# A split-precision feed-forward on one TensorE: within a weight tile, all products with the high parts first, then all with the low parts

## The chip, the core and the metric

The kernel runs on one core of one Trainium2 chip. The metric is the device time of one execution in microseconds (us). TensorE does the matrix products (PE in the profile; PEld is its weight load), VectorE is DVE, ScalarE is ACT, GpSimd is POOL, and SyncE (SP) issues most DMAs.

## The reference, cut to what matters

One layer of a hybrid model is computed for 128 context tokens and 512 latent tokens, 640 columns in all. The change lies in its last two pieces, the output projection and the feed-forward block:

```python
x = x + g1 * (jnp.concatenate([o_a, o_b], axis=-1) @ lp['w_out'])
h = _rmsnorm(x, lp['norm2_g']) * (1.0 + sc2) + sh2
ff = (jax.nn.silu(h @ lp['w_ffn_gate']) * (h @ lp['w_ffn_up'])) @ lp['w_ffn_down']
return x + g2 * ff, s_fin
```

The model width is 2048 and the feed-forward width is 5632. All inputs and outputs are 32-bit floats.

## The kernel before

**A product in three.** Each float matrix is split into a high part (a cast to the 32-bit format fp32r, in which TensorE takes it) and a low part (the matrix minus its high part). A product is the sum of three: high weight by high operand, high weight by low operand, low weight by high operand. The helper `parts` makes the weight's two parts: ACT casts `raw` to `hi` (line 1423), and DVE subtracts to get `lo` (line 1424). It does that once for a weight tile of `nk` blocks of 128x128 (`nk` is 4, or 3 in the first two chunks of the down projection). `hi`, `lo` and the sums `t3` of weights lie in the pool `st`, with three buffers each: a fourth `hi` can be written only when TensorE has read the first.

**Stages.** The output projection runs as two passes over 16 blocks of rows, one pass for each half of 320 columns (`hf` 0 and 1, lines 1482 to 1484). After each block, `add_out` adds the residual, `squares` takes squares of the new rows and sums them on POOL in groups of blocks, and `stats` multiplies a finished group with ones on TensorE (line 1462). After the last group of a half, `stats` also computes `rs`, the reciprocal root mean square of that half's columns (lines 1465 to 1467); `first_half` and `operand` turn the first half into TensorE's operands during the second pass.

The feed-forward block follows. `first_blocks` begins with plain products (`plain`, lines 1571 to 1573, accumulating in `C`) while the second half's operands are still made. Then the gate and up projections and the down projection run as seven products on sums of quarters (a Strassen-like scheme), each by `seven` (lines 1642 to 1644, accumulating in `P`). POOL subtracts weight tiles for it (line 1552). The gate and up operands are named `xo`, the down operands `xd`.

The down projection goes in six chunks of the inner dimension (`CHK`), and in each through eight pairs of output blocks. Where a chunk ends, the next chunk's operands are loaded from memory (`opd`), cast on ACT (line 1708) and subtracted on DVE, every fourth on POOL (line 1709); this stretch is called a turn here. There are five turns between chunks. The results are added into `acc` (line 1880). In the last chunk, `filled` copies `acc` back into a bank before the products (lines 2033 and 2034), and `Last` adds the residual x1d (line 1899).

**What sets the order.** A scheduler in the framework places the instructions of each engine's queue from the program's order and its own model of durations; each engine then runs its queue in order. TensorE's queue keeps the program's order of products. In `seven` the next tile's `parts` is asked for before the present tile's products.

The innermost loop before is

```python
TE.matmul(ps, hi[:, k, :], xk[:, 0, :], start=f, stop=False)
TE.matmul(ps, hi[:, k, :], xk[:, 1, :], start=False, stop=False)
TE.matmul(ps, lo[:, k, :], xk[:, 0, :], start=False, stop=l)
```

for each `k` in turn, so that the first use of `lo` is the third product of a tile and the last use of `hi` is the last but one.

Of the kernel before, what the change touches and what calls it, by code (L numbers as in the profile page):

```python
# [89 lines left out]
def flow_step(ctx: ExitStack, tc, x_prompt, x_sample, state_rwkv, c, c_ctx, w_mod, b_mod,  # L90
# [4 lines left out]
    V, S, G, TE = nc.vector, nc.scalar, nc.gpsimd, nc.tensor  # L95
# [427 lines left out]
    X = bz.tile([P, NCH, 2, CH], F32, name="X")  # L523
# [521 lines left out]
    def add_out(m, halves, hf=None):  # L1045

        for (lo, hi, v) in ((0, HALF, 0), (HALF, NLAT, 0), (NLAT, T, 1)):
            if hf is not None and lo // HALF != hf:
                continue
            dst = x1T[m][:, lo:hi]  # L1050
            o = HALF * (lo // HALF)
            V.scalar_tensor_tensor(out=dst, in0=halves[lo // HALF][:, lo - o:hi - o], scalar=modc[2][:, m, v:v + 1],
                                   in1=dst, op0=ALU.mult, op1=ALU.add)
# [307 lines left out]
    X = {}  # L1361
# [68 lines left out]
    with ExitStack() as ph:  # L1430
# [8 lines left out]
        sqs = []  # L1439
# [19 lines left out]
        def stats():  # L1459

            hf, m, sq = sqs.pop(0)
            TE.matmul(ss[hf], ones, sq, start=(m == GROUPS[hf][0][-1]), stop=(m == KB - 1))
            if m == KB - 1:
                s = slice(HALF * hf, HALF * hf + HALF)
                V.tensor_scalar(rs[:, s], ss[hf], 1.0 / D, RMS_EPS, op0=ALU.mult, op1=ALU.add)
                S.activation(rs[:, s], rs[:, s], AF.Sqrt)
                V.reciprocal(rs[:, s], rs[:, s])
# [3 lines left out]
        def four_blocks(hf, m, q):  # L1471

            s = slice(HALF * hf, HALF * hf + HALF)
            if q == 0:
                pool = pb2 if m % 2 or hf == 0 and m == 4 else pbig
                banks[m] = pool.tile([P, HALF], F32, tag="big", name="big")
            ps = banks[m]
            hi, lo = split(w_out[0, 4 * q * P:(4 * q + 4) * P, m * P:(m + 1) * P], 4,
                           *((wraw, wo) if q or hf or m >= AHEAD else ()))
            for k in range(4):  # L1480
                kb = 4 * q + k
                TE.matmul(ps, hi[:, k, :], o_hi[kb][:, s], start=(kb == 0), stop=False)  # L1482
                TE.matmul(ps, hi[:, k, :], o_lo[kb][:, s], start=False, stop=False)  # L1483
                TE.matmul(ps, lo[:, k, :], o_hi[kb][:, s], start=False, stop=(kb == 7))  # L1484
            return ps
# [3 lines left out]
        for hf in range(2):  # L1489
            s = slice(HALF * hf, HALF * hf + HALF)  # L1490
            for m in range(KB):
                if hf or m >= AHEAD:
                    four_blocks(hf, m, 0)
                ps = four_blocks(hf, m, 1)
                if hf and m in (6, 7, 8, KB - 1):
                    for _ in range(2):
                        next(first)
                if sqs and (sqs[0][1] >= 12 or m % 4 == 1):
                    stats()
                add_out(m, [ps, ps], hf)  # L1500
                nc.sync.dma_start(d_x1[m][:, s], x1T[m][:, s])
                squares(hf, m)
                if hf and m > 1:
                    for kb in HALVES[m - 2:m - 1] if m < 14 else HALVES[2 * m - 16:2 * m - 14]:
                        first_half(kb)
                    if 4 <= m < 12:
                        j, i = divmod(m - 4, 2)
                        operand(1 + i, j, x1T[j + 8 * i][:, t1])
        for i, raw in enumerate(held_w):
            hi, lo = (pre.tile([P, 4, P], F32R, tag=f"{t}{i}", name=t) for t in ("hi", "lo"))  # L1510
# [39 lines left out]
    def combined(out, a, b, nk=4):  # L1550
        for o, p, q in zip(out, a, b):
            G.tensor_tensor(out=o[:, 0:nk], in0=p[:, 0:nk], in1=q[:, 0:nk], op=ALU.subtract)  # L1552

    CP, DONE = {}, {}

    def plain(e):

        n, q, hs = PLAIN[e]
        for u in range(2):
            for b in range(2):  # L1560
                hi, lo = READY.pop(0) if READY else parts(PW.pop(0))
                next(loads, None)
                for h in hs:
                    if (n, u, h) not in CP:
                        CP[n, u, h] = pP.tile([P, 512], F32, tag="P", name="C")[:, 0:HALF]
                    ps, i = CP[n, u, h], ((1, 2), (5, 4))[h][b]
                    for k in range(4):
                        xk = X[i, 4 * q + k]
                        m = DONE.get((n, u, h), 0)
                        DONE[n, u, h] = m + 3  # L1570
                        TE.matmul(ps, hi[:, k, :], xk[:, 0, :], start=m == 0, stop=False)
                        TE.matmul(ps, hi[:, k, :], xk[:, 1, :], start=False, stop=False)
                        TE.matmul(ps, lo[:, k, :], xk[:, 0, :], start=False, stop=m == 45)

    def plain_out(n, h):

# [38 lines left out]
    def seven(b11, b12, b21, b22, x, hook, nk=4, bank=fresh, last=True, end=False):  # L1615

        def combine(out, a, b):
            combined(out, a, b, nk)
        t3 = [st.tile([P, 4, P], F32, tag="raw", name="t3", bufs=3) for _ in b11]
        combine(t3, b22, b12)  # L1620
        combine(b12, b12, b11)
        s6, s4 = b22, b21
        if end:
            s6, s4 = ([xap.tile([P, 4, P], F32, tag=next(wtags), name="rawd")] for _ in range(2))
            combine(s6, b22, b12)
            combine(s4, b21, s6)
        src = {1: b11, 2: b21, 3: b22, 7: t3, 5: b12, 6: s6, 4: s4}
        seq = PEND if end else PORD
        order = [raw for i in seq for raw in src[i]]

        ready = [parts(order.pop(0), nk)]
        for o, i in enumerate(seq):
            ps, filled = bank(i)
            nq = len(b11)
            for q in range(nq):
                hi, lo = ready.pop()
                if order:
                    ready.append(parts(order.pop(0), nk))
                for k in range(nk):
                    xk = x(i, 4 * q + k)  # L1640
                    f, l = q == 0 and k == 0 and not filled, q == nq - 1 and k == nk - 1 and last
                    TE.matmul(ps, hi[:, k, :], xk[:, 0, :], start=f, stop=False)  # L1642
                    TE.matmul(ps, hi[:, k, :], xk[:, 1, :], start=False, stop=False)  # L1643
                    TE.matmul(ps, lo[:, k, :], xk[:, 0, :], start=False, stop=l)  # L1644
            if i == 3 and not end:
                combine(b22, b22, b12)
                combine(b21, b21, b22)
            if last:
                hooks.append(lambda o=o, ps=ps: hook(o, ps))
            tick()  # L1650
            yield o
# [474 lines left out]
```

## Time and profile before

| | |
|---|---|
| median of 3 runs | 3223.48 us (3221.9 to 3225.47) |
| the profiled execution | 3213.3 us, of which 3211.5 us are the span |
| busy in the span | PE 3088.0, PEld 2858.2, DVE 2330.3, ACT 1460.1, POOL 1219.0 us |
| granted TensorE clock, mean | 0.991 |
| output projection, second pass | about 1449 to 1508 us of the span |
| first plain products | 1508 to about 1570 us |
| gate and up, seven products | about 1570 to 2606 us |
| down projection | about 2607 to 3196 us |

Times in the views are microseconds from the start of the span. A busy TensorE record of a matmul lasts longer than the distance to the next one, since their ends are modelled and they overlap; the pace is read from starts, not from durations. A row of the view of waits names who waited, the one that ended the wait, the total in us, the number of waits and the longest.

### The profile page before, as it was taken

To read this page: it belongs to the slowest core of one execution; us is meant where nothing else is said; L and a number is where in the kernel's file an instruction comes from. 1 tells how busy PE (TensorE), PEld (TensorE's weight loads), DVE (VectorE), ACT (ScalarE), POOL (GpSimd) and SP (SyncE) were. 2 spreads that over 40 slices of the span, in tenths; PEclk is the share of its full clock that TensorE was granted. 3 is DMA by queue.
4 is the path that set the end of the run, shared out by engine and by line. 5 is a ranking of instruction groups with operands and counts; after the bars stand their busy time and mean duration, and the time that the engine had idled before them with its cause. 6 is when DMAs were issued, how large, how long until landed. Compare 5 with 4: busy or idle time off the path is not lost.

```text
span 3211.5 us, 72260 instructions
## 1 busy us (share of the span) xinstructions
PE 3088.0 (96%) x28216; PEld 2858.2 (89%) x28216; DVE 2330.3 (73%) x4107; ACT 1460.1 (45%) x3197; POOL 1219.0 (38%) x1065
## 2 busy tenths in 40 slices
PE   6999989999999999999999999999999999999997
PEld 3688778788878888899999999999999999999997
DVE  4558666676657677767877777777777788887788
ACT  3344544454444444346644444444444454444365
POOL 2001121211122024311465566556655645555542
PEclk9999999999999999999999999999999999999999
DMA  9767786777778687564434434343344364553453
GB/s 372 239 187 203 210 215 171 209 218 193 201 198 216 210 275 253 173 200 133 141 116 130 127 105 123 118 124 118 113 128 126 104 199 152 159 165 112 140 165 122
DMA packets 740438, 550.88 MB, mean 172 GB/s; under 512 B 141056, under 2 KB 673504, under 8 KB 731264
## 3 DMA queue, kind: packets, MB, share of 16 engines
q1 hardware_dynamic: 727136, 532.47, 55.0%
q0 software_dynamic: 10624, 13.23, 1.9%
q8 instruction: 222, 3.64, 0.5%
q14 instruction: 120, 0.98, 0.1%
q10 hardware_dynamic: 2336, 0.57, 0.1%
HBM read 437.79 MB, written 110.95 MB: 171 GB/s over the span
## 4 chain that ended last, share of the span: by engine, by line
PE 56%; DVE 5%; issue 4%; DMA 3%; POOL 2%; ACT 2%; SPq 0%; DVEq 0%; POOLq 0%; ACTq 0%
PE P L1644 15%; PE P L1642 15%; PE P L1643 15%; DVE lo L1424 1%; PE big L1482 1%; PE big L1484 1%; PE big L1483 1%; PE big L1039 1%; PE big L190 1%; PE big L192 1%; PE big L191 1%; PE big L1041 1%; PE big L1040 1%; DMA opd<-d_op 1%; DMA rawd<-in_w_ffn_down_dram 1%
## 5 line engine op out<-in xcount | busy, mean ns | idle before, releaser
L1644 PE MATMUL P<-xo,lo 128*128 128x320 f32 x2352 | 727.1, 309 | 0.8 <-DVE lo L1424 0.7
L1642 PE MATMUL P<-xo,hi 128*128 128x320 f32 x2352 | 727.0, 309 | 0.7 <-ACT hi L1423 0.7
L1643 PE MATMUL P<-xo,hi 128*128 128x320 f32 x2352 | 726.9, 309 | 0.0
L1424 DVE TENSOR_TENSOR lo<-raw,hi 128x512 fp32r<-128x512 f32 x526 | 500.8, 955 | 174.4 <-ACT hi L1423 169.9
L1423 ACT CAST hi<-raw 128x512 fp32r<-128x512 f32 x526 | 326.7, 621 | 484.0 <-PE P L1643 392.1
L190 PE MATMUL big<-h_hi,hi 128*128 128x320 f32 x1376 | 447.3, 325 | 8.1 <-ACT hi L168 4.5
L1644 PEld LDWEIGHTS P<-xo,lo 128*128 128x128 f32 x2352 | 441.5, 188 | 1.8 <-DVE lo L1424 1.8
L1642 PEld LDWEIGHTS P<-xo,hi 128*128 128x128 f32 x2352 | 441.6, 188 | 1.0 <-ACT hi L1423 1.0
L1643 PEld LDWEIGHTS P<-xo,hi 128*128 128x128 f32 x2352 | 441.6, 188 | 0.0
L192 PE MATMUL big<-h_hi,lo 128*128 128x320 f32 x1376 | 431.1, 314 | 0.7 <-DVE lo L169 0.6
L191 PE MATMUL big<-h_lo,hi 128*128 128x320 f32 x1376 | 431.1, 313 | 0.7 <-DVE h_lo L352 0.4
L1552 POOL TENSOR_TENSOR raw<-raw 128x512 f32<-128x512 f32 x252 | 408.5, 1631 | 14.1 <-DVE lo L1424 2.7
L1644 PE MATMUL P<-xd,lo 128*128 128x320 f32 x1232 | 384.5, 312 | 16.3 <-DVE lo L1424 16.2
L1642 PE MATMUL P<-xd,hi 128*128 128x320 f32 x1232 | 382.7, 311 | 1.5 <-ACT hi L1423 0.3
L1643 PE MATMUL P<-xd,hi 128*128 128x320 f32 x1232 | 381.4, 310 | 0.0
L169 DVE TENSOR_TENSOR lo<-raw,hi 128x512 fp32r<-128x512 f32 x268 | 183.4, 689 | 200.6 <-ACT hi L168 185.1
L190 PEld LDWEIGHTS big<-h_hi,hi 128*128 128x128 f32 x1376 | 260.9, 190 | 58.1 <-issue 34.8
L1423 ACT CAST hi<-rawd 128x512 fp32r<-128x512 f32 (+1 forms) x288 | 168.8, 587 | 240.7 <-PE P L1643 203.1
L168 ACT CAST hi<-raw 128x512 fp32r<-128x512 f32 x268 | 164.5, 618 | 225.7 <-PE big L191 123.8
L191 PEld LDWEIGHTS big<-h_lo,hi 128*128 128x128 f32 x1376 | 261.3, 190 | 5.1 <-DVE h_lo L352 1.1
L192 PEld LDWEIGHTS big<-h_hi,lo 128*128 128x128 f32 x1376 | 260.3, 189 | 5.6 <-DVE lo L169 1.6
L1644 PEld LDWEIGHTS P<-xd,lo 128*128 128x128 f32 x1232 | 231.9, 188 | 23.2 <-DVE lo L1424 22.8
(404 smaller groups left out, 6052.8 us busy)
## 6 DMA issues: line engine op xcount, KB each, us to landing
wt<-in_w_mod_dram SPq DMA_DIRECT2D x96, 1024.0 KB
raw<-in_w_ffn_gate_dram SPq DMA_DIRECT2D x182, 256.0 KB
raw<-in_w_ffn_up_dram SPq DMA_DIRECT2D x182, 256.0 KB
rec<-d_S SPq DMA_DIRECT2D x80, 576.0 KB
raw<-in_w_in_dram SPq DMA_DIRECT2D x172, 256.0 KB
rawd<-in_w_ffn_down_dram SPq DMA_DIRECT2D x128, 256.0 KB
raw<-in_w_out_dram SPq DMA_DIRECT2D x96, 256.0 KB
xd<-d_os SPq DMA_DIRECT2D x66, 320.0 KB
```

The lines of the kernel that those rows point to most:

```text
L168: S.copy(hi, raw)
L169: V.tensor_sub(lo, raw, hi.bitcast(F32))
L190: TE.matmul(halves[hf], hi[:, k, :], h_hi[:, kb, s], start=(kb == 0), stop=False)
L191: TE.matmul(halves[hf], hi[:, k, :], h_lo[:, kb, s], start=False, stop=False)
L192: TE.matmul(halves[hf], lo[:, k, :], h_hi[:, kb, s], start=False, stop=(kb == KB - 1))
L1039: TE.matmul(halves[hf], hi[:, k, :], o_hi[kb][:, s], start=(k == 0), stop=False)
L1423: S.copy(hi[:, 0:nk], raw[:, 0:nk])
L1424: V.tensor_sub(lo[:, 0:nk], raw[:, 0:nk], hi[:, 0:nk].bitcast(F32))
L1552: G.tensor_tensor(out=o[:, 0:nk], in0=p[:, 0:nk], in1=q[:, 0:nk], op=ALU.subtract)
L1642: TE.matmul(ps, hi[:, k, :], xk[:, 0, :], start=f, stop=False)
L1643: TE.matmul(ps, hi[:, k, :], xk[:, 1, :], start=False, stop=False)
L1644: TE.matmul(ps, lo[:, k, :], xk[:, 0, :], start=False, stop=l)
```

## The change

In `plain` and `seven` a tile's products with `hi` all come first, two for each `k`, and its products with `lo` follow, one for each `k`. No product is added or dropped. The flag `stop` moves with the last product.

In the output projection, the rule that calls `stats` at once for groups that end at block 12 or later now holds for the second pass alone. So the first pass's last group (blocks 12 to 15), which was multiplied in the second pass's block 0, is multiplied in its block 1, and `rs` of the first half is computed there.

```diff
-                if sqs and (sqs[0][1] >= 12 or m % 4 == 1):
+                if sqs and (sqs[0][0] and sqs[0][1] >= 12 or m % 4 == 1):
                     stats()
...
                         TE.matmul(ps, hi[:, k, :], xk[:, 0, :], start=m == 0, stop=False)
                         TE.matmul(ps, hi[:, k, :], xk[:, 1, :], start=False, stop=False)
-                        TE.matmul(ps, lo[:, k, :], xk[:, 0, :], start=False, stop=m == 45)
+                    for k in range(4):
+                        TE.matmul(ps, lo[:, k, :], X[i, 4 * q + k][:, 0, :], start=False,
+                                  stop=DONE[n, u, h] == 48 and k == 3)
...
                 for k in range(nk):
                     xk = x(i, 4 * q + k)
-                    f, l = q == 0 and k == 0 and not filled, q == nq - 1 and k == nk - 1 and last
-                    TE.matmul(ps, hi[:, k, :], xk[:, 0, :], start=f, stop=False)
+                    TE.matmul(ps, hi[:, k, :], xk[:, 0, :], start=q == 0 and k == 0 and not filled, stop=False)
                     TE.matmul(ps, hi[:, k, :], xk[:, 1, :], start=False, stop=False)
-                    TE.matmul(ps, lo[:, k, :], xk[:, 0, :], start=False, stop=l)
+                for k in range(nk):
+                    TE.matmul(ps, lo[:, k, :], x(i, 4 * q + k)[:, 0, :], start=False,
+                              stop=q == nq - 1 and k == nk - 1 and last)
```

The changed file is three lines longer, so its line numbers are up to three higher: the products with `hi` are lines 1643 and 1644 there, those with `lo` line 1646, the cast of an operand 1711, its subtraction 1712, `add_out`'s counterpart in the last chunk (1899 before) 1902.

**TensorE, one tile of the down projection with four blocks.** Before, numbers of buffers kept:

```order
L1642 MATMUL P2_36586<-xd_36036,hi_36569 128x320
L1643 MATMUL P2_36586<-xd_36036,hi_36569 128x320
L1644 MATMUL P2_36586<-xd_36036,lo_36570 128x320
L1642 MATMUL P2_36586<-xd_36039,hi_36569 128x320
L1643 MATMUL P2_36586<-xd_36039,hi_36569 128x320
L1644 MATMUL P2_36586<-xd_36039,lo_36570 128x320
L1642 MATMUL P2_36586<-xd_36042,hi_36569 128x320
L1643 MATMUL P2_36586<-xd_36042,hi_36569 128x320
L1644 MATMUL P2_36586<-xd_36042,lo_36570 128x320
L1642 MATMUL P2_36586<-xd_36045,hi_36569 128x320
L1643 MATMUL P2_36586<-xd_36045,hi_36569 128x320
L1644 MATMUL P2_36586<-xd_36045,lo_36570 128x320
```

and the same tile after:

```order
L1643 MATMUL P2_36586<-xd_36036,hi_36569 128x320
L1644 MATMUL P2_36586<-xd_36036,hi_36569 128x320
L1643 MATMUL P2_36586<-xd_36039,hi_36569 128x320
L1644 MATMUL P2_36586<-xd_36039,hi_36569 128x320
L1643 MATMUL P2_36586<-xd_36042,hi_36569 128x320
L1644 MATMUL P2_36586<-xd_36042,hi_36569 128x320
L1643 MATMUL P2_36586<-xd_36045,hi_36569 128x320
L1644 MATMUL P2_36586<-xd_36045,hi_36569 128x320
L1646 MATMUL P2_36586<-xd_36036,lo_36570 128x320
L1646 MATMUL P2_36586<-xd_36039,lo_36570 128x320
L1646 MATMUL P2_36586<-xd_36042,lo_36570 128x320
L1646 MATMUL P2_36586<-xd_36045,lo_36570 128x320
```

The first product with `lo` moved from the third place to the ninth, the last with `hi` from the eleventh to the eighth.

**DVE, one turn of the down projection.** These are the rows in which the next chunk's operands are subtracted (`xd`) between the low parts of weights (`lo`). Before:

```order
L1424 TENSOR_TENSOR lo<-t_35955,hi 128x512
L1709 TENSOR_TENSOR xd<-opd,xd 128x320 x3
L1424 TENSOR_TENSOR lo<-rawd,hi 128x512 x2
L1709 TENSOR_TENSOR xd<-opd,xd 128x320 x4
L1424 TENSOR_TENSOR lo<-rawd,hi 128x512
L1709 TENSOR_TENSOR xd<-opd,xd 128x320
L1424 TENSOR_TENSOR lo<-rawd,hi 128x512
L1709 TENSOR_TENSOR xd<-opd,xd 128x320 x3
L1424 TENSOR_TENSOR lo<-rawd,hi 128x512 x2
```

After, from the same row `t_35955`:

```order
L1424 TENSOR_TENSOR lo<-t_35955,hi 128x512
L1424 TENSOR_TENSOR lo<-rawd,hi 128x512
L1712 TENSOR_TENSOR xd<-opd,xd 128x320 x3
L1424 TENSOR_TENSOR lo<-rawd,hi 128x512 x2
L1712 TENSOR_TENSOR xd<-opd,xd 128x320 x3
L1424 TENSOR_TENSOR lo<-rawd,hi 128x512 x2
L1712 TENSOR_TENSOR xd<-opd,xd 128x320 x3
L1424 TENSOR_TENSOR lo<-rawd,hi 128x512
```

One more low part stands ahead of the first three subtractions of operands, and no more than three of those stand together. Two of the eleven subtractions have left the stretch; they come later.

**ACT in the same turn**, where the operands are cast (`xd`) between the high parts of weights (`hi`). Before:

```order
L1423 CAST hi<-t_35955 128x512
L1708 CAST xd<-opd 128x320 x3
L1423 CAST hi<-rawd 128x512
L1708 CAST xd<-opd 128x320
L1423 CAST hi<-rawd 128x512
L1708 CAST xd<-opd 128x320 x4
L1423 CAST hi<-rawd 128x512
L1708 CAST xd<-opd 128x320 x2
```

After:

```order
L1423 CAST hi<-t_35955 128x512
L1423 CAST hi<-rawd 128x512
L1711 CAST xd<-opd 128x320 x4
L1423 CAST hi<-rawd 128x512 x2
L1711 CAST xd<-opd 128x320 x4
L1423 CAST hi<-rawd 128x512 x2
```

The casts of operands now stand in groups of four, with two high parts of weights behind each group.

**DVE in the last chunk**, once for each pair of output blocks. Before:

```order
L1424 TENSOR_TENSOR lo<-rawd,hi 128x512
L1926 TENSOR_TENSOR cd<-P_38836,tp 128x320
L1424 TENSOR_TENSOR lo<-rawd,hi 128x512
L1899 SCALAR_TENSOR_TENSOR cd<-cd,modc_90,x1d 128x192
L1899 SCALAR_TENSOR_TENSOR cd<-cd,modc_90,x1d 128x128
L1424 TENSOR_TENSOR lo<-t_38874,hi 128x512
L1899 SCALAR_TENSOR_TENSOR cd<-cd,modc_90,x1d 128x192
L1899 SCALAR_TENSOR_TENSOR cd<-cd,modc_90,x1d 128x128
L1910 TENSOR_TENSOR cd<-P_38881,tp 128x320
L1424 TENSOR_TENSOR lo<-rawd,hi 128x512 x2
```

After:

```order
L1424 TENSOR_TENSOR lo<-rawd,hi 128x512 x2
L1929 TENSOR_TENSOR cd<-P_38836,tp 128x320
L1424 TENSOR_TENSOR lo<-t_38874,hi 128x512
L1902 SCALAR_TENSOR_TENSOR cd<-cd,modc_90,x1d 128x192
L1902 SCALAR_TENSOR_TENSOR cd<-cd,modc_90,x1d 128x128
L1902 SCALAR_TENSOR_TENSOR cd<-cd,modc_90,x1d 128x192
L1902 SCALAR_TENSOR_TENSOR cd<-cd,modc_90,x1d 128x128
L1424 TENSOR_TENSOR lo<-rawd,hi 128x512
L1913 TENSOR_TENSOR cd<-P_38881,tp 128x320
L1424 TENSOR_TENSOR lo<-rawd,hi 128x512
```

The four residual additions of a pair, which stood two and two around a low part, now stand together behind three low parts.

## The prediction

> **What bounds the kernel now.** I read the page's busy times first, then the busy time of each engine by stage, then who waited for whom on TensorE, and last the order of time on DVE around the longest waits.
>
> The page's first part, with each engine's share of the span:
>
> ```profile
> PE 3088.0 (96%) x28216; PEld 2858.2 (89%) x28216; DVE 2330.3 (73%) x4107; ACT 1460.1 (45%) x3197; POOL 1219.0 (38%) x1065
> ```
>
> TensorE sets the time. The next view has stretches of the span, their length, busy times and granted clock: the second output pass, the first plain products, gate and up, the start of the down projection, its chunks, and its last chunk.
>
> ```profile
> core 0: us, PE busy (x) PEld busy (x) DVE busy (x) ACT busy (x) POOL busy (x), PEclk, DMA share, GB/s
> 1449.00:1508.00 59.00, 57.65 (x380) 55.84 (x378) 41.66 (x88) 36.84 (x73) 14.43 (x10) 1.00 0.47 142
> 1508.00:1575.00 67.00, 62.00 (x410) 60.16 (x411) 62.45 (x130) 49.02 (x113) 12.24 (x5) 1.00 0.48 139
> 1575.00:2590.00 1015.00, 1015.00 (x6922) 1015.00 (x6921) 772.90 (x973) 440.35 (x770) 616.58 (x415) 1.00 0.40 120
> 2607.00:2640.00 33.00, 29.61 (x185) 28.36 (x185) 25.64 (x41) 16.00 (x37) 17.59 (x16) 0.95 0.68 215
> 2640.00:2760.00 120.00, 118.22 (x800) 116.93 (x798) 95.93 (x165) 57.20 (x124) 64.37 (x56) 1.00 0.45 137
> 2760.00:3086.00 326.00, 319.34 (x2162) 316.97 (x2162) 257.20 (x378) 134.94 (x246) 172.52 (x115) 1.00 0.51 155
> 3086.00:3196.00 110.00, 102.98 (x687) 97.45 (x685) 94.33 (x150) 71.72 (x204) 37.09 (x25) 1.00 0.31 92
> ```
>
> In gate and up TensorE never pauses (1015.00 of 1015.00): a better order has nothing to give there. In the plain products and the down projection it does pause. For whom, says the view of TensorE's waits from 1505 us to 3196 us, its largest three rows:
>
> ```profile
> PE P L1644 <- DVE lo L1424: 16.9, 23, 1.5
> PE C L1573 <- DVE lo L1424: 3.1, 3, 1.7
> ...
> PE P L1642 <- ACT hi L1423: 1.1, 2, 0.7
> ```
>
> Nearly all of it is the wait that the change aims at: a tile's third product, the first with the low part, waits for DVE. A high part is waited for twice.
>
> **The change part by part.**
>
> *The pace, and what one wait costs.* The next row is that of the gate and up products with low parts, with their number, durations and first and last start; behind it stand such products around the start of the down projection, in order of time.
>
> ```profile
> L1644 PE MATMUL P<-xo,lo x2352: 303/309/418, 1569.7 to 2606.5; 128*128 128x320 f32 x196
> ...
> 2612.23 0.41 PE L1644 MATMUL P<-xd,lo 128*128 128x320 f32 x1 [1.14 <-DVE lo L1424]
> ...
> 2615.93 0.41 PE L1644 MATMUL P<-xd,lo 128*128 128x320 f32 x1 [1.50 <-DVE lo L1424]
> ...
> 2617.50 0.47 PE L1644 MATMUL P<-xd,lo 128*128 128x320 f32 x1
> 2618.30 0.47 PE L1644 MATMUL P<-xd,lo 128*128 128x320 f32 x1
> ...
> 2619.90 0.47 PE L1644 MATMUL P<-xd,lo 128*128 128x320 f32 x1
> ```
>
> Three times 2352 products in 1036.8 us are one each 0.147 us, while a record lasts 0.309. So a wait in these rows begins 0.16 us after the pace was lost, and the waiting product's record is 0.1 us longer (0.41). Each of the 26 waits costs 0.26 us more than its row: 20.0 + 26 x 0.26 = 26.8 us. That is all that this edit can take from TensorE's waits for low parts. Besides, after the two waits above, nine products from 2617.50 take 2.40 us instead of 1.32, with the stretch's clock at 0.95: another 1.1 us.
>
> *What the new order gives each tile.* With four blocks the low part is due at the ninth product instead of the third: 6 x 0.147 = 0.88 us later (with three blocks at the seventh: 0.59 us). A high part's buffer is free three products earlier, 0.44 us (two, 0.29 us). That reaches DVE only where ACT was waiting for the buffer, as in this row of ACT's waits from 2590 us to 3196 us, against which the second holds up the casts for DMAs:
>
> ```profile
> ACT hi L1423 <- PE P L1643: 242.5, 246, 2.6
> ...
> ACT xd L1708 <- DMA opd<-d_op: 20.4, 12, 3.2
> ```
>
> The number and length of products, casts and subtractions stay. Now stage by stage; the waits that fall into the four windows, each from the same view:
>
> ```profile
> PE C L1573 <- DVE lo L1424: 3.1, 3, 1.7
> PE P L1644 <- DVE lo L1424: 0.7, 2, 0.5
> ...
> PE P L1644 <- DVE lo L1424: 3.0, 3, 1.5
> ...
> PE P L1644 <- DVE lo L1424: 8.2, 10, 1.2
> ...
> PE P L1644 <- DVE lo L1424: 4.9, 8, 0.9
> ```
>
> They are 1508 to 1576 us (two rows), 2590 to 2640, 2640 to 3086, and 3086 to 3196 us.
>
> *First plain products:* five waits, 3.8 + 1.3 = 5.1 us. But DVE is busy 62.45 of 67 us; it makes operands and low parts together, and a later deadline only shifts the wait. The last tile gains the 0.88 us by which its low part is due later and about one operand's subtraction that the scheduler has put behind it. I take 1.5 us, between 0.9 and 5.1.
>
> *Start of the down projection:* three waits, 3.0 + 0.8 = 3.8 us, and the slow 1.1 us. DVE just before them:
>
> ```profile
> 2609.28 1.63 DVE L1818 TENSOR_TENSOR act<-act,c 128x640 f32<-128x640 f32 x1
> 2610.83 1.35 DVE L1424 TENSOR_TENSOR lo<-t,hi 128x384 fp32r<-128x384 f32 x1
> 2612.10 1.15 DVE L1709 TENSOR_TENSOR xd<-opd,xd 128x320 fp32r<-128x320 f32 x1
> 2613.18 2.22 DVE L1779 TENSOR_TENSOR act<-act,sp 128x320 fp32r<-128x320 f32 x2
> ```
>
> The second wait (1.50) stands behind the last two rows; in the new order that low part precedes both, and the wait goes. The low part behind them is late instead, by about 0.9 us. The first wait (1.14) gets an operand's subtraction more ahead of it and 0.59 us of delay: it stays at about 1 us with its 0.26. So 4.9 - 0.9 - 1.3 = 2.7 us, between 0 and 4.9.
>
> *Chunks:* ten waits, 8.2 + 2.6 = 10.8 us. In the turn that the order shows, DVE runs
>
> ```profile
> 2855.26 0.69 DVE L1424 TENSOR_TENSOR lo<-t,hi 128x512 fp32r<-128x512 f32 x1 [1.06 <-ACT hi L1423]
> 2855.87 4.18 DVE L1709 TENSOR_TENSOR xd<-opd,xd 128x320 fp32r<-128x320 f32 x3
> 2859.97 1.28 DVE L1424 TENSOR_TENSOR lo<-rawd,hi 128x512 fp32r<-128x512 f32 x2
> ...
> 2865.76 1.28 DVE L1709 TENSOR_TENSOR xd<-opd,xd 128x320 fp32r<-128x320 f32 x3
> 2866.97 1.97 DVE L1424 TENSOR_TENSOR lo<-rawd,hi 128x512 fp32r<-128x512 f32 x2
> ```
>
> and the low part at 2859.97 ends a wait. After, it stands ahead of the 4.18 us; the next is due one tile and 0.88 us later, 2.6 us in all, and only 0.6 us of DVE's work is between them. The longest wait, 1.2 + 0.16, is near 0.88 + 0.44. I take 9 us, between 5 and 10.8.
>
> *Last chunk:* eight waits, 4.9 + 2.1 = 7.0 us. DVE around the wait that the order shows:
>
> ```profile
> 3099.92 1.78 DVE L1424 TENSOR_TENSOR lo<-rawd,hi 128x512 fp32r<-128x512 f32 x1
> ...
> 3102.03 0.68 DVE L1424 TENSOR_TENSOR lo<-rawd,hi 128x512 fp32r<-128x512 f32 x1
> 3102.62 1.71 DVE L1899 SCALAR_TENSOR_TENSOR cd<-cd,modc,x1d 128x192 f32<-128x192 f32 x2
> ```
>
> The longest, 0.9 + 0.16, nearly fits into 0.88. But two of the 1.71 us now stand together, 3.4 us ahead of the third next low part; counting on from 3102.6 it is ready about 0.3 us late, six times over, 2 us. I take 5 us, between 2 and 7.
>
> *The squares:* a multiplication of 320 columns moves past 24 products, 3.5 us, and so do `rs` and the operands behind it. DVE idles 17 of the 59 us of that pass, where TensorE pauses 1.35 us in all; the idle time hides the move. I take nothing, with up to 3.5 us lost if that cover were gone and up to 1.35 us gained.
>
> *The sum:* 1.5 + 2.7 + 9 + 5 = 18.2 us. The profiled execution took 3213.3 us; it becomes 3195.1. The median of the runs is 10.2 us above the profiled execution, and I carry that over: 3205.3 us.
>
> Of the slow products at 2617 the Trainium skill, "TensorE: Matmul & The Clock Gate", Part 1, says that the clock halves after an idle window of about 3.4 us whose phase is free. By that rule the 1.1 us hang on chance as long as one of the two waits stays, and the sum would be 17.1 us without them; the trace shows the slow stretch once among 26 waits.
>
> **The rivals.**
>
> *Little gained, DVE is the limit.* If every burst on DVE only pushes its wait to a later tile, each gives the 0.88 us once: the plain products, the start and five turns, 7 x 0.88 = 6.2 us, with nothing from the last chunk: 3217.3 us. For it speaks DVE's 62.45 of 67 us; against it the chunks, where DVE has 69 of 326 us idle. Chance 0.12.
>
> *Slower: high parts late behind the casts of operands.* In a turn ACT now runs four casts of operands ahead of two high parts. Where those casts wait for their DMA (12 times, up to 3.2 us), both high parts wait, and TensorE stops at the tile's first product, which no order of products cushions. With one tile of 1.76 us in hand, a stop costs up to 3.2 - 1.76 + 0.26 = 1.7 us; three groups in each of five turns are 25.5 us, against 18.2 gained: 3230.8 us. It takes eleven of the fifteen groups to decide. Against it: the rows have 12 such waits in all, most of them shorter than the tile in hand. Chance 0.07.
>
> *Slower: low parts meet POOL.* The low part of 512 columns takes 0.69 us at 2855.26 and 1.78 at 3099.92; the three subtractions of operands 1.28 us and 4.18. POOL was subtracting weights beside the long ones:
>
> ```profile
> 2853.67 4.94 POOL L1552 TENSOR_TENSOR rawd<-rawd 128x512 f32<-128x512 f32 x3
> ```
>
> If each of the 26 low parts, at its new time, met POOL, it would come 1.1 us later, more than the 0.88 us: 26 x 1.1 - 18.2 = 10.4 us slower, 3233.9 us. It decides from 17 of 26. Against it: the waits are those where the meeting has happened already. Chance 0.04. The Trainium skill, "SBUF — State Buffer", section "Who interferes with whom", makes it a lock: whichever of the two starts first holds the shared ports to its end; the rows at 2853.67 and 2855.87 agree.
>
> That the change does nothing is excluded: the order shows the low parts moved in every tile.
>
> **How the numbers follow.** The forecast has 0.77, the rivals 0.12, 0.07 and 0.04. Its own bounds are the sums of the stages' bounds, 8 and 27.8 us gained, so 3195.7 to 3215.5. The range reaches up to the first rival and some way beyond, 3195 to 3221 us. About 0.2%, 6.4 us, is what a measurement of this kernel can tell from no change; the first rival's 6.2 us fall within it. So faster 0.77, same 0.12, slower 0.11.
>
> **What would show it right or wrong.** Right: the waits of the product with `lo` fall from 20.0 us to under 7, gate and up stay without a pause, the clock of the down projection's start rises from 0.95. A wrong step shows as waits for `hi` above 5 us (second rival), as waits for `lo` that moved to other tiles (first), or as low parts with a longer mean duration (third). Pauses in the second output pass would mean that the squares were not hidden. The prediction falls if the median is above 3217.

## The result and the profile after

| | before | after |
|---|---|---|
| median of 17 runs each, same chip | 3225.47 us (3221.48 to 3232.46) | 3215.22 us (3207.18 to 3222.47) |
| ratio, 95% interval | | 0.9966 [0.9957, 0.9974] |
| the profiled execution | 3213.3 us, span 3211.5 | 3217.6 us, span 3215.9 |

By the ratio the change takes 11.0 us (8.4 to 13.9) off the time of before; the medians lie 10.3 us apart. The direction was forecast, the size was not: 18.2 us were forecast.

The two profiled executions say the opposite, 4.3 us slower, and must be read by stretches. TensorE's products can be counted: each trace has 28216 of them, so the start of the n-th one can be compared. Up to product 16400 (in the output projection) no line is changed, and in the fourteen profiles of this document that part, counted from the first product, takes 1415.5 to 1429.8 us. Before's profile has the shortest, 1415.5; after's has 1423.3. This 7.8 us says nothing of the change.

The same part of the page, after:

```profile
PE 3098.5 (96%) x28216; PEld 2872.4 (89%) x28216; DVE 2333.0 (73%) x4107; ACT 1459.9 (45%) x3197; POOL 1223.9 (38%) x1065
```

The stretches of after that answer to those of before, some 3 to 8 us later in the span: the second output pass, gate and up (from 1590 us on), the start of the down projection (from 2610 us), its chunks (from 2645) and its last chunk (from 3090).

```profile
1456.79:1515.79 59.00, 57.65 (x380) 55.83 (x378) 41.98 (x88) 36.49 (x73) 12.98 (x10) 1.00 0.47 142
1590.00:2600.00 1010.00, 1010.00 (x6888) 1010.00 (x6887) 774.38 (x968) 438.68 (x766) 622.90 (x410) 1.00 0.40 120
2610.00:2645.00 35.00, 32.13 (x215) 31.25 (x214) 28.01 (x47) 17.29 (x39) 16.05 (x14) 1.00 0.83 260
2645.00:2764.00 119.00, 115.80 (x778) 113.85 (x777) 92.14 (x161) 55.07 (x121) 62.43 (x56) 1.00 0.44 133
2764.00:3090.00 326.00, 324.33 (x2203) 322.81 (x2202) 257.64 (x385) 137.33 (x254) 175.75 (x118) 1.00 0.51 158
3090.00:3200.00 110.00, 103.24 (x693) 99.78 (x691) 93.09 (x150) 73.72 (x203) 37.74 (x26) 0.98 0.31 92
```

In the second output pass, taken 7.79 us later as its products come, TensorE is busy for 57.65 us with 380 products, as before. In the chunks' two stretches together TensorE now pauses 4.9 us instead of 8.4 (3.20 and 1.67, before 1.78 and 6.66; the cuts do not fall at quite the same product). In the last chunk it pauses as before: 103.24 of 110 us busy, 102.98 before. The clock there has fallen to 0.98.

TensorE's waits in the whole down projection of after, 2590 to 3196 us (in us: total, number, longest):

```profile
PE P L1646 <- DVE lo L1424: 4.8, 9, 0.9
PE P L1643 <- ACT P L2037: 3.1, 2, 2.0
PE P L1643 <- ACT hi L1423: 2.9, 3, 1.3
PE P L2036 <- DVE cd L1918: 2.4, 5, 1.0
PE P L1643 <- DVE acc L1881: 1.1, 1, 1.1
```

The waits for low parts in the down projection fell from 16.1 (the start's 3.0, the chunks' 8.2, the last chunk's 4.9) to 4.8 us. But four rows stand beside them whose lines had next to nothing before: 9.5 us of waits for a bank that is filled or freed late, and for high parts. 5.5 us of them are the last chunk's (lines 2037 and 1918).

### The profile page after: what moved, and what is told of

It is laid out like the page before. It is cut to its first block, busy times and chain, and to the rows that moved or that the text cites. A ratio compares the mean times of both kernels' runs of the same rounds, so it can differ in the third digit from the quotient of the medians.

```text
span 3215.9 us, 72260 instructions
## 1 busy us (share of the span) xinstructions
PE 3098.5 (96%) x28216; PEld 2872.4 (89%) x28216; DVE 2333.0 (73%) x4107; ACT 1459.9 (45%) x3197; POOL 1223.9 (38%) x1065
## 4 chain that ended last, share of the span: by engine, by line
PE 56%; DVE 6%; issue 4%; DMA 3%; POOL 2%; ACT 1%; SPq 0%; DVEq 0%; POOLq 0%; ACTq 0%
PE P L1646 15%; PE P L1643 15%; PE P L1644 15%; DVE lo L1424 1%; PE big L1482 1%; PE big L1483 1%; PE big L1484 1%; PE big L1039 1%; PE big L190 1%; PE big L192 1%; PE big L191 1%; PE big L1041 1%; PE big L1040 1%; DMA ol<-d_o 1%; DMA opd<-d_op 1%
## 5 line engine op out<-in xcount | busy, mean ns | idle before, releaser
L1643 PE MATMUL P<-xo,hi 128*128 128x320 f32 x2352 | 699.9, 309 | 0.1
L1644 PE MATMUL P<-xo,hi 128*128 128x320 f32 x2352 | 699.8, 309 | 0.0
L1424 DVE TENSOR_TENSOR lo<-raw,hi 128x512 fp32r<-128x512 f32 x526 | 517.8, 990 | 163.8 <-ACT hi L1423 162.0
L1646 PE MATMUL P<-xo,lo 128*128 128x320 f32 x2352 | 441.3, 309 | 3.1 <-DVE lo L1424 3.1
L1643 PE MATMUL P<-xd,hi 128*128 128x320 f32 x1232 | 368.5, 310 | 7.1 <-ACT P L2037 3.1
L1646 PEld LDWEIGHTS P<-xo,lo 128*128 128x128 f32 x2352 | 369.4, 188 | 4.0 <-DVE lo L1424 4.0
L1644 PE MATMUL P<-xd,hi 128*128 128x320 f32 x1232 | 367.5, 310 | 0.0
L169 DVE TENSOR_TENSOR lo<-raw,hi 128x512 fp32r<-128x512 f32 x268 | 184.4, 693 | 201.4 <-ACT hi L168 186.0
L1552 POOL TENSOR_TENSOR t<-raw 128x512 f32<-128x512 f32 x84 | 123.9, 1475 | 427.7 <-DMA raw<-in_w_ffn_up_dram 419.2
L1424 DVE TENSOR_TENSOR lo<-rawd,hi 128x512 fp32r<-128x512 f32 (+1 forms) x288 | 227.0, 795 | 25.4 <-ACT hi L1423 24.6
```

What stands on the lines that cost most here:

```text
L169: V.tensor_sub(lo, raw, hi.bitcast(F32))
L1424: V.tensor_sub(lo[:, 0:nk], raw[:, 0:nk], hi[:, 0:nk].bitcast(F32))
L1643: TE.matmul(ps, hi[:, k, :], xk[:, 0, :], start=q == 0 and k == 0 and not filled, stop=False)
L1646: TE.matmul(ps, lo[:, k, :], x(i, 4 * q + k)[:, 0, :], start=False, stop=q == nq - 1 and k == nk - 1 and last)
```

## The experiments

Each was timed beside the kernel before on the same chip. The table has the ratio with its interval and, from one profile each, the time between the starts of four products: 24000 (in gate and up, 57 us before the down projection), 24800 (67 us into it), 27200 (48 us before the last chunk) and the last one. The three stretches are called start, chunks and last.

| kernel | ratio | start | chunks | last | sum |
|---|---|---|---|---|---|
| before | | 124.0 | 364.0 | 158.8 | 646.8 |
| e_stats | 0.9997 [0.9981, 1.0012] | 123.9 | 367.4 | 158.2 | 649.6 |
| e_plain | 1.0002 [0.9991, 1.0014] | 124.4 | 365.5 | 158.7 | 648.5 |
| e_gu | 1.0007 [0.9996, 1.0018] | 125.1 | 365.4 | 158.0 | 648.5 |
| after | 0.9966 [0.9957, 0.9974] | 123.5 | 358.7 | 158.4 | 640.6 |
| e_down | 0.9960 [0.9944, 0.9976] | 123.1 | 358.0 | 158.2 | 639.3 |
| d_x1 | 0.9978 [0.9965, 0.9990] | 123.1 | 357.9 | 159.7 | 640.8 |
| d_tp | 0.9982 [0.9973, 0.9991] | 123.8 | 358.5 | 160.3 | 642.6 |
| d_early | 1.0000 [0.9989, 1.0010] | 124.8 | 360.7 | 159.7 | 645.2 |
| d_late | 0.9974 [0.9962, 0.9987] | 123.7 | 355.7 | 155.7 | 635.1 |
| d_xb | 0.9953 [0.9936, 0.9970] | 123.7 | 359.4 | 153.1 | 636.2 |
| d_xbtp | 0.9962 [0.9949, 0.9975] | 123.7 | 358.4 | 151.8 | 634.0 |
| l_xbtp | 0.9951 [0.9936, 0.9966] | 123.7 | 356.9 | 153.1 | 633.7 |
| b_xbtp | 1.0000 [0.9989, 1.0012] | 123.6 | 367.0 | 157.7 | 648.3 |

The ratios tell kernels apart by some 4 us at best, the stretches by 1 to 3: the four kernels with the old order in the down projection and its old buffers agree within 2.8 us there, the three with the new order and the old buffers in effect (after, e_down, d_x1) within 1.5.

### Which part of the change pays

**e_stats**: the first hunk alone.

```diff
-                if sqs and (sqs[0][1] >= 12 or m % 4 == 1):
+                if sqs and (sqs[0][0] and sqs[0][1] >= 12 or m % 4 == 1):
```

> Only the squares are moved: the first half's last group is multiplied a block later, all products keep the old order. Forecast's theory (idle time of DVE hides it): within 0.1% of before, and no new pause of TensorE in the second output pass. Rival (the move frees TensorE there, so that part of the whole change's 0.34% comes from here): 1 to 3 us faster, with the pauses of the second pass gone. Rival on the other side (operands come later): the waits at the first plain products grow by 1 to 3.5 us.

Nothing: 0.9997, and the stretch from product 16400 to 17000 takes 92.5 us in this kernel as in before. The interval leaves room for 6 us less or 4 more; the stretch does not.

**e_plain**: the hunk in `plain` alone, **e_gu** and **e_down**: the new order in `seven` for gate and up, or for the down projection, by one condition.

```diff
+                if nq == 1:      # e_down; e_gu has nq == 2
+                    ...          # the order of after
+                else:
+                    ...          # the order of before
```

> The new order in the first plain products alone. Forecast's theory: 1.5 us faster (0.05%), waits for low parts there fall from 3.8 us to under 3. What the profile of the whole change suggests instead: the wait only moves behind them, to the first tiles of gate and up, and TensorE loses up to 3 us there: 0 to 0.1% slower.

> The new order in gate and up alone, all else as before. Forecast's theory: TensorE never pauses there, so nothing is gained: within 0.1%. Rival (the order itself changes the pace of the products, or the first tiles of gate and up lose by the new order): the pace differs from 0.147 us for a product, or a wait of 2 us appears in the first tile: up to 0.1% slower; a pace that is 1% better would give 10 us.

> The new order in the down projection alone. Forecast's theory: nearly the whole gain is here, 16.7 of 18.2 us, so at least as fast as the whole change: 11 to 16.7 us faster than before (0.34 to 0.52%). Rival (DVE is the limit and each burst only moves its wait): about 6 us (0.19%). If the whole change's loss against the forecast lies in the plain products, this kernel is about 3 us faster than the whole change.

The whole gain is in the down projection. e_down alone has 0.9960, the whole change 0.9966. The plain products and gate and up have 1.0002 and 1.0007, with nothing within their intervals. Products 18000 to 24000 take 880.0 us in all fourteen profiles, 0.1467 us each: the order does not change the pace. In e_plain the waits of TensorE from 1540 to 1605 us are

```profile
PE P L1646 <- DVE lo L1424: 3.1, 3, 2.3
PE C L1574 <- DVE lo L1424: 2.1, 1, 2.1
```

against 2.2 (line 1573) and 0.7 us (line 1644) in before: the wait is larger and most of it stands at the first tiles behind the plain products. Little of that is shown to be the new order's, though: e_stats, with the old order there, has 2.4 and 2.0 us, for a reason told in the last section. By the stretches the down projection gains 1.1 us at the start, 7.4 in the chunks, and loses 0.3 in the last stretch (means of the four old and three new kernels): 8.2 us. The interval of the whole change begins at 8.4; where the other 2 to 3 us of its 11.0 lie, no profile showed.

### A later deadline or an earlier release

The new order does two things: the low part is due later, and the high part's buffer is free earlier. d_early keeps the second (in a tile of four blocks the last product with the high part is the ninth, against the eighth in e_down and the eleventh before), d_late the first (the first product with the low part is the eighth, against the ninth in e_down and the third before).

```diff
                     TE.matmul(ps, hi[:, k, :], xk[:, 1, :], start=False, stop=False)
+                    if k == 0:
+                        TE.matmul(ps, lo[:, 0, :], xk[:, 0, :], start=False, stop=False)
-                for k in range(nk):
+                for k in range(1, nk):
                     TE.matmul(ps, lo[:, k, :], x(i, 4 * q + k)[:, 0, :], ...
```

> As e_down (the new order in the down projection alone), but each tile's first product with the low part is back at the third place; the other low parts stay last. The low part is due as early as before, while the high part's buffer comes free as early as in e_down. Forecast's theory (the later deadline takes the waits): the waits for low parts come back, 15 us or more of them, and the gain goes: within 0.1% of before. Rival (the gain comes from the earlier release of the high part and from where low parts now stand on DVE): the waits for low parts stay under 6 us and it is as fast as e_down, 0.4% faster than before.

```diff
-                    TE.matmul(ps, hi[:, k, :], xk[:, 1, :], start=False, stop=False)
+                    if k < nk - 1:
+                        TE.matmul(ps, hi[:, k, :], xk[:, 1, :], start=False, stop=False)
...
+                TE.matmul(ps, hi[:, nk - 1, :], xk[:, 1, :], start=False, stop=False)
+                TE.matmul(ps, lo[:, nk - 1, :], xk[:, 0, :], start=False, stop=q == nq - 1 and last)
```

> As e_down, but one product with the high part is kept back to the last place but one, where it was before: the low part is due late, the high part's buffer comes free as late as before. Forecast's theory (the deadline alone): as fast as e_down, about 13 us faster than before (0.4%). Rival (the earlier release does it): within 0.1% of before, and ACT waits for the buffer as long as before (242.5 us in all) instead of less.

The waits for low parts in the down projection, in d_early, in e_down and in d_late:

```profile
PE P L1646 <- DVE lo L1424: 14.3, 17, 1.6
```

```profile
PE P L1645 <- DVE lo L1424: 3.1, 6, 0.9
```

```profile
PE P L1647 <- DVE lo L1424: 4.0, 7, 1.2
```

With the first low part due at the third product again, most of the waits are back, 14.3 us, and no gain is measured: 1.0000. Yet DVE's queue in d_early is almost that of e_down: 52 of some 4100 instructions stand elsewhere. d_late, in which the high part is kept as long as before, has the gain: 0.9974, and 635.1 us in its stretches, 4.2 less than e_down; and its DVE queue is nearer to that of before (53 places differ) than to that of e_down (97). So the gain follows the deadline, and neither the earlier release nor e_down's places on DVE are needed for it.

That these two bring nothing is not shown. By stretches d_early, with 645.2 us, is still 3.1 us shorter than the mean of the four kernels with the old order, and the interval of its ratio leaves room for 3.5. It comes from the chunks, which take 360.7 us against 364.0 to 367.4, in one profile of d_early. The waits for low parts there, from 2640 to 3090 us, first in before, then in d_early:

```profile
PE P L1644 <- DVE lo L1424: 9.0, 11, 1.2
```

```profile
PE P L1646 <- DVE lo L1424: 5.8, 9, 1.1
```

Beside the later deadline the earlier release rather seems to cost: e_down takes 2.3 us more than d_late in the chunks and 2.5 more in the last stretch, in one profile each. DVE's and ACT's orders differ between these two as well (97 and 67 places), so this cost can't be put down to the release alone. Nor does ACT's wait for the buffer, by which d_late's rival was to be known, tell the two apart: in the down projection it is 242.5 us in before, 210.4 in d_early, 206.1 in d_late and 188.6 in e_down.

### Where the last chunk's gain went

After's last stretch takes 158.4 us, before's 158.8, though the waits for low parts there fell from 4.9 to 0.6 us. From 3060 to 3200 us, DVE's waits for x1d in before, after and e_down:

```profile
DVE cd L1899 <- DMA x1d<-d_x: 9.9, 7, 1.9
```

```profile
DVE cd L1902 <- DMA x1d<-d_x: 13.3, 7, 2.4
```

```profile
DVE cd L1908 <- DMA x1d<-d_x: 12.9, 7, 2.5
```

and ACT's waits for tp, in the same order:

```profile
ACT tp L1909 <- DVE cd L1926: 5.4, 5, 2.2
```

```profile
ACT tp L1912 <- DVE cd L1929: 8.9, 5, 4.0
```

```profile
ACT tp L1918 <- DVE cd L1935: 12.0, 6, 3.5
```

In after's order of time on DVE, one pair:

```profile
3110.03 2.30 DVE L1902 SCALAR_TENSOR_TENSOR cd<-cd,modc,x1d 128x192 f32<-128x192 f32 x4
...
3116.08 0.55 DVE L1902 SCALAR_TENSOR_TENSOR cd<-cd,modc,x1d 128x320 f32<-128x320 f32 x1 [2.15 <-DMA x1d<-d_x]
3116.55 1.29 DVE L1424 TENSOR_TENSOR lo<-rawd,hi 128x512 fp32r<-128x512 f32 x2
3117.76 0.48 DVE L1918 TENSOR_TENSOR cd<-P,cd 128x320 f32<-128x320 f32 x1
```

The four residual additions now end together at 3112.3. They hold the buffers of x1d nearly until then (SP issues the next pair's DMA from 3111.77 on), so that DMA starts late, and DVE waits for it with two low parts and the sum that frees TensorE's bank (line 1918) queued behind; the fill product (line 2036) waits for that bank. At the start of the last chunk ACT waits in the same manner for tp, the buffer that DVE's last sum of the pair must have read:

```profile
3093.45 0.43 ACT L1912 COPY tp<-P 128x320 f32<-128x320 f32 x1 [3.98 <-DVE cd L1929]
3093.77 0.62 ACT L1423 CAST hi<-rawd 128x512 fp32r<-128x512 f32 x1
3094.29 0.43 ACT L2037 COPY P<-acc 128x320 f32<-128x320 f32 x1
```

and the copy that fills a bank comes 2 us late for TensorE. Two kernels were to tell the two waits apart.

**d_x1**, the first addition asked for later; **d_tp**, a second buffer for tp:

```diff
                 V.tensor_add(self.cs[0][:, t1], ps[2], tp[:, 0])
-                self.out(0, 0)
...
                 V.tensor_add(act[:, t1], ps[3], act[:, t2])
+                self.out(0, 0)
```

> As e_down, and in the last chunk the first residual addition of a pair (the one that waits for the DMA of x1d, 11.1 us in six waits) is asked for after the product sums that free the bank. Theory: this DMA wait on DVE is what makes TensorE's fill products wait for line L1924 (4.2 us, five times, and the slow stretches behind them); these waits go, and it is 3 to 5 us faster than e_down (0.5% faster than before). Rival (DVE has too much to do in the last chunk, wherever it waits): as e_down, with the lost time under another name.

```diff
-                self.tp = tp = xap.tile([P, 2, HALF], F32, tag="rs2", name="tp")
+                self.tp = tp = dn.tile([P, 2, HALF], F32, tag="tp", name="tp", bufs=2)
```

> As e_down, and in the last chunk the tile tp has a second buffer of its own, so that ACT's copy into it need not wait for DVE's last sum of the pair before (12.0 us in six waits in e_down, 5.4 before). Theory: the two stops of TensorE of 1.3 and 1.7 us behind a fill copy go: 2 to 4 us faster than e_down. Rival (those waits have slack, and the x1d wait or DVE's own work sets the pace): as e_down within 0.1%.

d_x1 tells nothing of its theory: the scheduler put the addition back where it had been, ahead of the sum, and the kernel is e_down once more, with the same instructions in the same order on DVE, ACT and POOL. It shows instead how far two runs of one kernel lie apart: 640.8 and 639.3 us by stretches, 0.9978 and 0.9960 by ratio. d_tp removes ACT's wait for tp and gains nothing, 160.3 us in the last stretch; its fill products wait 5.5 us for line 1924 instead of 4.2, and DVE waits 15.7 us for x1d instead of 12.9. So tp is not the first limit. x1d was tried next, with a second buffer for that of a pair's first block (**d_xb**), then both (**d_xbtp**, where the freed place serves tp):

```diff
-            xqs[n] = [xap.tile([P, T], F32, tag=f"x1_{(1, 9)[m]}", name="x1d") for m in range(2)]
+            xqs[n] = [dn.tile([P, T], F32, tag="x1d", name="x1d", bufs=2), xap.tile([P, T], F32, tag="x1_9", name="x1d")]
...                                                        # d_xbtp:
-                self.tp = tp = xap.tile([P, 2, HALF], F32, tag="rs2", name="tp")
+                self.tp = tp = xap.tile([P, 2, HALF], F32, tag=("rs2", "x1_1")[n % 2], name="tp")
```

> As e_down, and x1d of the first block of a pair has two buffers, so that its DMA need not wait until the pair before has read it. In e_down SP holds this DMA back until line L1908 is done, and DVE then waits 11.1 us in six waits for its landing. Theory: these waits are what delays the sums that free TensorE's banks; the waits of DVE for x1d fall under 3 us, those of the fill products (4.2 us) under 1.5, and the stretch from product 27200 to the last (158.2 us in e_down) gets 3 to 5 us shorter. Rival (ACT's wait for tp, 12.0 us, sets the pace): the DVE waits go and the stretch stays above 157.

> As d_xb, and tp takes two buffers in turn. Theory: with both waits gone the last chunk gives what the forecast wanted of it: from product 27200 to the last 153 to 155 us instead of 158.2. Rival (DVE has too much work in a pair): above 157, with TensorE waiting for DVE under other names.

TensorE's waits from 3083 to 3200 us in d_xb, then in d_xbtp:

```profile
PE P L1642 <- ACT P L2043: 2.0, 2, 1.5
PE prd L2014 <- ACT junk L2018: 1.4, 1, 1.4
PE P L1645 <- DVE lo L1424: 0.4, 1, 0.4
```

```profile
PE P L1645 <- DVE lo L1424: 1.1, 3, 0.5
```

With x1d in time, the fill products no longer wait, and the last stretch takes 153.1 us, 5.1 less than in e_down; with tp as well it takes 151.8. That is the 5 us that the forecast wanted of the last chunk.

**l_xbtp** has d_late's order with both buffers, **b_xbtp** the old order with both.

> The order of d_late (one product with the high part kept back to the last place but one), with the two buffers for x1d and for tp. Theory (the later deadline gains, the earlier release of the high part costs in chunks and last chunk): from product 24000 to the last under 634 us, and 13 to 17 us faster than before (0.4 to 0.5%), the fastest of all. Rival (d_late's 635.1 us in its profile was chance): 637 to 641 us, as d_xbtp.

> The order of before everywhere, with the two buffers for x1d and for tp. Theory (before, low parts were the last to come, x1d and tp were hidden): from product 27200 to the last 157 to 159 us as before, the whole within 0.1%. Rival (these waits cost in the old order too): 2 to 4 us shorter, and then the gain of the other kernels in the last chunk is not that of the new order.

In the old order the buffers bring nothing: 1.0000, 157.7 us in the last stretch. x1d and tp became the last to come only when the low parts no longer were. l_xbtp is the shortest of all, with 633.7 us and 0.9951, but d_xbtp has 634.0: with the buffers in place d_late's advantage in the last chunk is gone, and 1.5 us of that in the chunks are left. By ratio l_xbtp and d_xb are the fastest, 15.8 and 15.2 us off before (medians 3207.87 and 3207.79 us); their intervals overlap each other's and that of the whole change, which ran on another occasion, so only the stretches say that they beat it: 633.7 and 636.2 us against 640.6.

## Why the prediction was right, and where it was off

**The mechanism** held. TensorE's waits for low parts were the time to be had, and the later deadline takes them: they fell from 20.0 to 9.0 us over the whole feed-forward (4.8 in the down projection, 2.4 and 1.8 around the plain products' end). "Under 7" was named for the whole, and was missed. d_early and d_late show that the gain follows the deadline. The share that the prediction gave to the earlier buffer was not needed; a part of the chunks' gain may still be its, or that of the new order on DVE, as d_early's chunks suggest.

**Gate and up** was right: 1010.00 of 1010.00 us busy, and the same 880.0 us for 6000 products in all kernels. **The squares** were right: TensorE's pauses in the second pass are the same 1.35 us of 59, and e_stats shows nothing.

**Chunks**, 9 us taken: 7.4 measured, within its bounds. Of what is missing, the waits for high parts show 1.7 us in two waits: where a tile's low part is no longer late, its high part sometimes is.

**Start of the down projection**, 2.7 us taken: 1.1 measured. The three waits for low parts are still there with 2.4 us, as the first and the one behind were said to be. The clock rose from 0.95 to 1.00 as named, but that was luck: in e_down, with the same order there, it is at half for 3.41 us from 2619.1 us on. What the term left out is 1.1 us each for line 1881 and for a high part in that stretch.

**First plain products**, 1.5 us taken: nothing, between 3 us gained and 4.5 lost by e_plain's interval. The step "a later deadline only shifts the wait" should have been followed to its end, to the first tile of gate and up, where after waits 2.4 us. How much of that the change shifted there is not shown: in seven of the eleven profiles with the old order TensorE waits 1.9 us at that tile too, and from product 17000 to 18000 after takes 155.9 us, as they do.

**Last chunk**, 5 us taken: -0.3 measured. This is the term that was mis-sized. The step "two of the 1.71 us now stand together" asked only what the group does to the next low parts, 0.3 us six times. It did not ask what else hangs on the group: the buffers of x1d, whose DMA SP holds back until the group is done; the sum that frees a bank, behind that DMA on DVE; and tp. Those waits were on the profile of before, 9.9 and 5.4 us on DVE and ACT, and looked harmless because neither reached TensorE. They reached it as soon as the low parts were in time: the second buffer for x1d gives 5.1 us in the new order (d_xb), and both buffers give nothing in the old one (b_xbtp). That tp costs something of its own is less sure: 1.3 us from d_xb to d_xbtp, nothing in d_tp.

So the sum was 8.2 us by stretches and 11.0 by the ratio, against 18.2. Of the 10 us between the forecast and the stretches, 5.3 are the last chunk's, 1.6 the chunks', 1.6 the start's and 1.5 the plain products'. The time itself, 3215.22 us against 3205.3, is 9.9 us off, of which 2.0 are the median of before, 3225.47 us here and 3223.48 in the prediction. It lies in the range because the range was drawn past the first rival's 3217.3 us.

**The rivals.** That DVE is the limit and each burst gives 0.88 us once, 6.2 us in all: not in the chunks, which gave 7.4 alone; but in the plain products and the last chunk the waits did move to other tiles and other lines, and there it was nearer than the forecast. In size both 8.2 and 11.0 us lie nearer to this rival than to the forecast; the time alone would not have told the two apart, the chunks do. High parts late behind operand casts: 2.9 us in the whole down projection against the 5 us named, no. Low parts meeting POOL: in the down projection the mean of the 288 low parts of loaded tiles (`rawd`) went from 800 to 795 ns, that of the 132 of sums of weights, a part of them in gate and up, from 1052 to 1130; the rival needed 1.1 us on each of 17, no.

## What to carry to other kernels

When a wait is to be removed, list for each engine behind it what is next late, its buffers and their DMAs too: the waits of other engines that do not reach the bound now are the price list of the change. An order of products that needs a late tile last is worth having only where that tile was the last to come, and the second buffer that lets it pay may be worth nothing without it (b_xbtp 1.0000, d_xb 0.9953). Where executions of unchanged code differ by 14 us, count the bound engine's instructions and compare stretches, before the total.

## What the runs showed of the hardware

**One order, two times.** From product 17000 to 18000 (the plain products and the first tiles of gate and up) kernels with the old order there take either 153.0 to 153.6 us (four profiles, before among them) or 155.9 to 156.9 (seven); e_down and d_x1, 153.5 and 156.0 us, have the same instructions there. In before, DVE runs through while POOL is held up; a row of each:

```profile
1572.13 4.08 POOL L1758 TENSOR_TENSOR s<-act 128x320 f32<-128x320 f32 x1 [6.06 <-DVE xo L1382]
1572.77 0.69 DVE L1424 TENSOR_TENSOR lo<-raw,hi 128x512 fp32r<-128x512 f32 x1
```

In e_stats the same two rows come out the other way:

```profile
1576.58 1.05 POOL L1758 TENSOR_TENSOR s<-act 128x320 f32<-128x320 f32 x1 [6.06 <-DVE xo L1382]
1577.90 1.34 DVE L1424 TENSOR_TENSOR lo<-raw,hi 128x512 fp32r<-128x512 f32 x1
```

POOL takes 1.05 us instead of 4.08, DVE's low part 1.34 instead of 0.69, and TensorE's wait at the first tile of gate and up is 1.9 us instead of 0.5. All eleven profiles divide like this: POOL's row takes 4.08 us in the four short ones and 1.05 or 1.06 in the seven long ones. The Trainium skill, "SBUF — State Buffer", section "Who interferes with whom", has the two share ports under an exclusive lock; these rows agree in that each is slow where the other is not, and some 3 us of a kernel hang on it. What decides is not shown: in both cases POOL's row starts 0.16 us after a row of DVE did.

**A slow clock after short stops.** In e_stats TensorE is stopped twice for the same 1.87 us:

```profile
1569.43 0.41 PE L1573 MATMUL C<-xo,lo 128*128 128x320 f32 x1 [1.87 <-DVE lo L1424]
1569.68 0.31 PE L1571 MATMUL C<-xo,hi 128*128 128x320 f32 x1
1569.83 0.30 PE L1572 MATMUL C<-xo,hi 128*128 128x320 f32 x1
...
1579.30 0.63 PE L1644 MATMUL P<-xo,lo 128*128 128x320 f32 x1 [1.87 <-DVE lo L1424]
1579.73 0.47 PE L1642 MATMUL P<-xo,hi 128*128 128x320 f32 x1
1580.00 0.47 PE L1643 MATMUL P<-xo,hi 128*128 128x320 f32 x1
```

After the first the products go on at 0.147 us, after the second at 0.267, ten of them, for 1.2 us lost. What tells the two apart is how the idle time falls into a grid. From 1505 to 3190 us the granted clock falls to half 33 times in the fourteen profiles, for 3.41 us each time but one (6.83), and within a profile these stretches begin at whole multiples of 3.41 us from each other. If the span is cut into pieces along that grid, TensorE was idle for 1.56 to 2.42 us of the piece before each of the 33. After a piece with less than 1.56 us idle the clock never fell; between 1.56 and 1.68 us it fell or did not. The pieces around the two stops of e_stats, with TensorE's busy time first and the clock third from the end:

```profile
1565.44:1568.85 3.41, 2.12 (x15) 1.85 (x13) 3.41 (x3) 0.63 (x2) 3.31 (x3) 1.00 0.42 130
1568.85:1572.27 3.42, 2.36 (x14) 2.09 (x15) 3.42 (x7) 1.78 (x4) 1.62 (x1) 1.00 0.40 125
1575.68:1579.09 3.41, 1.04 (x6) 0.51 (x4) 3.41 (x6) 2.58 (x6) 2.35 (x3) 1.00 0.37 118
1579.09:1582.51 3.42, 3.21 (x12) 3.21 (x13) 3.42 (x5) 0.41 (x1) 1.88 (x2) 0.50 0.36 102
```

The first stop is divided between two pieces, 1.29 us idle in the one; the second lies nearly whole in one piece, with another stop of 0.72 us, 2.37 us idle together. The prediction saw one such stretch in before; after has three, behind stops of 1.80, 2.42 and 1.97 us, and e_gu none. The Trainium skill, "TensorE: Matmul & The Clock Gate", Part 1, has the clock at half after an idle window of about 3.4 us whose phase is free. The grid agrees in length and in the free phase; that half a window's idle time was enough here differs from the page.
